# MoE weights fetched 1024 columns wide, its experts reordered into long stretches, the first expert's overflow slots packed

## The chip, the cores and the metric

The kernel runs on one core of a Trainium2 chip, in one launch. The metric is the device time in microseconds (us), here of that one core. Engines are named as the profile names them: PE is TensorE (PEld its weight loads), DVE VectorE, ACT ScalarE, POOL GpSimd, SP SyncE, which issues nearly all weight loads.

## What is computed

A block of two layers runs on 256 tokens of width 1024, all in float32; a second block of two layers follows. The first block has SwiGLU layers around a mixer of delta rule, convolution and attention. The second has a short convolution, a SwiGLU, a dilated attention and last a mixture of experts (MoE). Every normalisation of the second block is shifted and scaled by vectors that come from `silu(c) @ mod_w` ("modulation"). The change lies in the MoE, with one edit in the modulation:

```python
def swiglu_2(h, w_gate, w_up, w_down):
    return (jax.nn.silu(h @ w_gate) * (h @ w_up)) @ w_down

def moe_swiglu(h, w_router, w_gate, w_up, w_down):      # 8 experts, each 1024 -> 2816 -> 1024
    top_val, top_idx = lax.top_k(h @ w_router, 2)       # every token goes to two experts
    ...
    for e in range(N_EXPERTS):
        out = out + gates[..., e:e + 1] * swiglu_2(h, w_gate[e], w_up[e], w_down[e])
```

## The kernel before

**Weights and precision.** Outside the Half experts (below) a float32 product is made of fp32r matmuls: a weight piece of 128x1024 is split into `wh` (a copy, ACT, L197) and `wl` (the rest, DVE, L198) by `Core.parts`; the activations are split likewise. `mm3` then adds three matmuls: high by high, high by low, low by high. Activations are the stationary operand, weights the moving one. `Core.load` (L175) fetches up to 1 MB of weights per DMA (L187) on SP's queue into a ring of buffers, six of 1 MB in the MoE (`K.more(3)` adds three to three); `parts` writes into a ring of four pairs.

**The experts.** `Experts.route` ranks the eight experts by how many tokens chose them, on the chip; position 0 is the fullest, 7 the emptiest. `Experts.gather` (L1629) picks the tokens of up to three positions with one-hot matmuls. Three sorts of work follow.
- `Slots` (positions 0 to 3): up to 128 tokens, three fp32r matmuls of 512 columns per 128 rows of weight and 512 columns.
- `Half` (positions 4 to 7, and the tokens of position 0 beyond 128): up to 64 tokens. Its weights are not split; `halves` (L254) issues two plain fp32 matmuls with 64 stationary columns, which write rows 0 to 63 and rows 64 to 127 of one PSUM bank. The trace shows each as two records. The result lies as two halves of the columns, one under the other, and `feat` (L1454) copies and transposes gate and up, each on its own.
- An `If` at the end for counts beyond these.

`Experts.expert` (L1675) runs one position: for every 512 of the 2816 columns the gate products, then the up products (`proj_tok`, L259: loads of 4x128 rows by 512 columns, so rows of 2 KB), then `rows` (L303) for the down product (loads of 2x128 rows by 1024 columns, rows of 4 KB). It is a generator, which yields after each column chunk and after each down load. The PSUM banks are seven for products (`acc`) and one for transposes (`tr`).

**The order.** `moe` (L1691) writes the order of work with `beside`, which alternates two generators: position 0 (with its overflow) beside 7 and then 6; position 1 beside 5; position 2 beside 4; position 3 alone. So three of the four stages mix a Slots expert with a Half one, changing over after every chunk and, in the down products, after every load. Inside position 0 the Slots matmuls and the Half matmuls of the overflow alternate at every 128x1024 piece. The framework orders each engine's instructions by a simulated time line that starts from this order, so the trace shows the order it chose; each engine then runs its list in that order.

**The modulation.** `modulation` (L1128) is stepped once per weight load in three of the first block's SwiGLU stages. For each 512 of its columns it loads four pieces of `mod_w` on POOL's queue, adds them up on DVE (`macc`), and, right after the fourth (`k0 == 6`), splits the sum into `mh` and `ml` and sums it over the partitions with two matmuls into the bank `pm`; there are 24 such groups.

Of the kernel before, what the change touches and what calls it, by code (L numbers as in the profile page):

```python
# [18 lines left out]
P = 128  # L19
# [68 lines left out]
class Core:  # L88
# [170 lines left out]
    def proj_tok(self, xs, W, c0, n, kts, done, also=()):  # L259


# [4 lines left out]
        for k0 in range(0, kts, kc):  # L266
            m = min(kc, kts - k0)
            w = self.load([W[k0 * P:(k0 + m) * P, c].rearrange("(k p) n -> p k n", p=P) for c in cols], m, n)
            for j0 in range(0, m, kp):
                piece = w[:, j0:min(m, j0 + kp)]  # L270
                split = [] if self.raw(xs) else self.parts(piece)
                for t, x in enumerate(xs):
                    for j in range(piece.shape[1]):
                        k = k0 + j0 + j
                        ends = k == 0, k == kts - 1
                        if isinstance(x, Raw):
                            self.halves(ps[t], x(k), piece[:, j], n // 2, *ends)
                        else:
                            self.product(ps[t][:, :n], x, k, [v[:, j] for v in split], *ends)
        for t, x in enumerate(xs):  # L280
            done(t, ps[t][:, :n // 2 if isinstance(x, Raw) else n])
# [846 lines left out]
def modulation(K, part):  # L1128
# [19 lines left out]
    ahead = load(*pieces[0])  # L1148
    yield
    for n, (r, c0, k0) in enumerate(pieces):  # L1150
# [16 lines left out]
        if k0 == 6:  # L1167
            h, l = (pool.tile([P, 512], F32R, name=x, bufs=1) for x in ("mh", "ml"))
            K.split(acc, h, l)
            ps = K.bank("pm")  # L1170
            K.mm(ps, one, h, True, False)
            K.mm(ps, one, l, False, True)
            out = acc[0:1]
            nc.vector.tensor_tensor(out, ps[0:1], vec[:, 0], op=ALU.add)
            if j == 1:
                nc.vector.scalar_tensor_tensor(out, out, 1.0, vec[:, 1], op0=ALU.add, op1=ALU.mult)
            nc.gpsimd.dma_start(K.mods[r:r + 1, c0:c0 + 512], out)
        if n % 2:
            yield

# [200 lines left out]
class Slots:  # L1381
# [13 lines left out]
    def gate(self, ps, n):  # L1395
        self.g = self.E.tmp.tile([P, 512], F32, tag="sg", name="sg")
        self.nc.scalar.activation(self.g[:, :n], ps, AF.Silu)

    def up(self, ps, n, k0):
        K, m = self.K, n // P  # L1400
        self.nc.vector.tensor_tensor(self.g[:, :n], self.g[:, :n], ps, op=ALU.mult)
        tp = heads(K.tr(), 4)
        for j in range(m):
            K.transpose(tp[:, j], self.g[:, j * P:(j + 1) * P])
        K.split(tp[:, :m], self.h[:, k0:k0 + m], self.l[:, k0:k0 + m])

    def down(self, ps):
# [3 lines left out]
        for half in range(2):  # L1411
            c = slice(half * 512, half * 512 + 512)
            y = ps[half]
            if E.ending:
                y = E.tmp.tile([P, 512], F32, tag="sg", name="y")
                nc.vector.tensor_tensor(y, ps[half], E.scale[:, c], op=ALU.mult)
            K.split(y, yh[:, c], yl[:, c])
        pm, tp = E.tmp.tile([P, 2, P], F32, tag="pmd", name="pmd", bufs=1), heads(K.tr(), 4)
        for t in range(2):
            E.onehot(pm[:, t], self.slot, t, self.pos)  # L1420
            K.transpose(tp[:, t], pm[:, t])
        pt = E.tmp.tile([P, 2, P], F32R, tag="pt", name="pt")
# [8 lines left out]
        E.fresh = False  # L1431

# [10 lines left out]
class Half(Slots):  # L1443
# [20 lines left out]
    def gate(self, ps, n):  # L1464
        g = self.E.tmp.tile([P, 256], F32, tag="hg", name="hg")[:, :n // 2]
        self.g = g.rearrange("p (h j s) -> p h j s", h=2, s=64)
# [345 lines left out]
```

## Time and profile before

| | us |
|---|---|
| median of 3 runs (2684.63 to 2686.72) | 2685.23 |
| the profiled execution's own time | 2684.64 |
| its span, first to last instruction | 2682.8 |
| PE busy in the span | 2584.4 (96%) |
| DVE busy | 1738.8 (65%) |
| ACT busy | 1226.8 (46%) |

HBM read is 630.18 MB, 235 GB/s over the span. How to read a profile of this kind: busy time is the union of the records of an engine; matmuls are pipelined, so a record is longer than the step from one start to the next, and the step is what an engine's pace is read from. A wait line says which engine stood idle and what ended it. A window line has, for a stretch of time, the busy time of each engine with its number of records, the granted TensorE clock, the mean busy share of the 16 DMA engines and the GB/s moved. A few matmul records can be missing.

### The profile page before, as it was taken

The page shows a single profiled execution, that of the slowest core. Times are in us where ns is not written, and L with a number is a line of the kernel's source. Part 1 is how long each engine was busy: PE and PEld are TensorE (multiplying, and loading weights), DVE is VectorE, ACT ScalarE, POOL GpSimd, SP SyncE. Part 2 cuts the span into 40 slices and gives each one's busy share as a digit, 9 for nine tenths or more (in the row PEclk, how much of TensorE's full clock was granted, in tenths as well). Part 3 has the DMA queues.
Part 4 walks back from the last instruction along what each step waited for, and adds up shares of the span by engine and source line. Part 5 has one row for each costly group of instructions (what it writes and reads, how often), then busy time and mean ns, then how long its engine had stood idle before and what let it go on. Part 6 is the DMA issues. An engine that isn't in the chain of part 4 may idle for free. (4 is left out here: it accounts for less than half of the span.)

```text
span 2682.8 us, 37809 instructions
## 1 busy us (share of the span) xinstructions
PE 2584.4 (96%) x14817; PEld 2069.5 (77%) x14817; DVE 1738.8 (65%) x2490; ACT 1226.8 (46%) x1771; POOL 168.4 (6%) x259
## 2 busy tenths in 40 slices
PE   8999999999999999999999999997999999999997
PEld 6889999777778899988879788785556556666566
DVE  7868798887786688875556554765333355455487
ACT  5436545444444564454435443453322234434466
POOL 1210100122120010000000000001000000000000
PEclk9999999999999999999999999998999999999999
DMA  8865435787786552456555555424887989999995
GB/s 320 288 240 171 127 111 161 247 283 274 252 287 222 169 160 81 153 182 215 180 190 195 181 188 188 144 78 177 328 336 280 336 317 381 362 364 363 370 344 204
DMA packets 310678, 633.82 MB, mean 236 GB/s; under 512 B 16428, under 2 KB 107548, under 8 KB 310492
## 3 DMA queue, kind: packets, MB, share of 16 engines
q1 hardware_dynamic: 294876, 580.87, 61.6%
q0 software_dynamic: 15616, 50.46, 5.6%
q8 instruction: 118, 1.93, 0.3%
q14 instruction: 68, 0.56, 0.1%
HBM read 630.18 MB, written 1.10 MB: 235 GB/s over the span
## 5 line engine op out<-in xcount | busy, mean ns | idle before, releaser
L198 DVE TENSOR_TENSOR wl<-w,wh 128x1024 fp32r<-128x1024 f32 (+2 forms) x818 | 976.2, 1208 | 440.0 <-ACT wh L197 436.2
L197 ACT ACTIVATE wh<-w 128x1024 fp32r<-128x1024 f32 (+2 forms) x818 | 842.8, 1047 | 699.9 <-PE acc L202 539.2
L202 PE MATMUL acc<-wh,xh 128*128 128x512 f32 (+4 forms) x1584 | 605.6, 384 | 9.7 <-ACT xh L215 4.2
L202 PE MATMUL acc<-wl,xh 128*128 128x512 f32 (+4 forms) x1584 | 607.2, 383 | 7.3 <-DVE wl L198 7.2
L202 PE MATMUL acc<-wh,xl 128*128 128x512 f32 (+4 forms) x1584 | 600.0, 380 | 6.3 <-DVE xl L216 6.1
L202 PEld LDWEIGHTS acc<-wh,xh 128*128 128x128 f32 x1584 | 304.2, 192 | 79.6 <-issue 10.7
L202 PEld LDWEIGHTS acc<-wl,xh 128*128 128x128 f32 x1584 | 304.6, 192 | 73.8 <-DVE wl L198 13.7
L202 PEld LDWEIGHTS acc<-wh,xl 128*128 128x128 f32 x1584 | 304.8, 192 | 61.2 <-DVE xl L216 10.2
L202 PE MATMUL acc<-xh,wl 128*128 128x256 f32 x864 | 247.4, 286 | 0.0
L202 PE MATMUL acc<-xh,wh 128*128 128x256 f32 x864 | 247.1, 286 | 0.0
L202 PE MATMUL acc<-wl,ah 128*128 128x512 f32 x616 | 246.8, 401 | 0.3 <-DVE wl L198 0.3
L202 PE MATMUL acc<-xl,wh 128*128 128x256 f32 x864 | 245.4, 284 | 0.0
L202 PE MATMUL acc<-wh,al 128*128 128x512 f32 x616 | 241.9, 394 | 0.0
L202 PE MATMUL acc<-wh,ah 128*128 128x512 f32 x616 | 230.6, 398 | 0.0
L202 PE MATMUL acc<-w,xr 128*64 128x256 f32 (+1 forms) x1920 | 229.9, 367 | 0.0
L202 PEld LDWEIGHTS acc<-w,xr 128*64 128x64 f32 x1920 | 131.1, 136 | 78.0 <-issue 31.6
L202 PEld LDWEIGHTS acc<-xh,wh 128*128 128x128 f32 x864 | 165.4, 191 | 0.7 <-issue 0.5
L202 PEld LDWEIGHTS acc<-xl,wh 128*128 128x128 f32 x864 | 165.1, 191 | 0.6 <-issue 0.5
L202 PEld LDWEIGHTS acc<-xh,wl 128*128 128x128 f32 x864 | 165.1, 191 | 0.1
L1166 DVE SCALAR_TENSOR_TENSOR macc<-wm,vec,macc 128x512 f32<-128x512 f32 x168 | 125.1, 745 | 46.4 <-DMA wm<-in_mod_w_dram 45.0
L202 PEld LDWEIGHTS acc<-wl,ah 128*128 128x128 f32 x616 | 115.8, 188 | 50.3 <-issue 13.5
L202 PEld LDWEIGHTS acc<-wh,ah 128*128 128x128 f32 x616 | 114.4, 188 | 33.0 <-ACT wh L197 4.1
(414 smaller groups left out, 2749.5 us busy)
## 6 DMA issues: line engine op xcount, KB each, us to landing
w<-in_moe_w_gate_dram SPq DMA_DIRECT2D x88, 1024.0 KB
w<-in_moe_w_up_dram SPq DMA_DIRECT2D x88, 1024.0 KB
w<-in_moe_w_down_dram SPq DMA_DIRECT2D x88, 1024.0 KB
w<-in_ffn_w_gate_dram SPq DMA_DIRECT2D x55, 1024.0 KB
w<-in_ffn_w_up_dram SPq DMA_DIRECT2D x55, 1024.0 KB
w<-in_ffn_w_down_dram SPq DMA_DIRECT2D x55, 1024.0 KB
wm<-in_mod_w_dram POOLq DMA_DIRECT2D x96, 512.0 KB, 5.8
w<-in_w_in_dram SPq DMA_DIRECT2D x48, 1024.0 KB
```

What stands on the lines that cost most here:

```text
L197: self.nc.scalar.activation(like(h), v, AF.Copy)
L198: self.nc.vector.tensor_tensor(like(l), v, like(h).bitcast(F32), op=ALU.subtract)
L202: self.nc.tensor.matmul(out=out, lhsT=l, rhs=r, start=start, stop=stop)
L1166: nc.vector.scalar_tensor_tensor(acc, w[:, k], sc, acc, op0=ALU.mult, op1=ALU.add)
```

## The change

It has five parts.
1. `wide` takes the place of `proj_tok` in the experts: gate and up go in chunks of 1024, 1024 and 768 columns, loads of 2x128 rows by 1024 (or 768) columns, so rows of 4 KB (3 KB). A Slots job takes two PSUM banks for a chunk, a Half job one.
2. `Half` applies silu to the bank of the gate product as it lies, multiplies by the bank of the up product, and transposes the product once, up to four blocks in a bank, instead of gate and up apart, two blocks in a bank.
3. The overflow of position 0 is `Packed`: its 64 token columns of high part and 64 of low part stand side by side as one stationary operand of 128 columns, so that two fp32r matmuls (by `wh` and by `wl`) of 512 columns take the place of four fp32 records; `feat` then transposes and adds the two halves of the rows.
4. The order: position 0 with its overflow still alternates with 7 and 6, but by chunks of gate or of up (4 MB) and by four down loads; then 5, 1, 2, 3 and 4 run one behind the other. There are five gathers instead of four.
5. In `modulation` the two `pm` matmuls of a group and what follows them move to the next group's second piece (`k0 == 2`), and the small vectors are loaded at `k0 == 4`. Some scratch tiles share tags ("sg" with three buffers).

```diff
+    def wide(self, xs, W, c0, n, done):
+        pieces = [[slice(0, n // 2)] if isinstance(x, Raw) else [slice(c, min(n, c + 512)) for c in range(0, n, 512)]
+                  for x in xs]
+        ps = [[self.acc()[:, :c.stop - c.start] for c in cs] for cs in pieces]
+        for k0 in range(0, 8, 2):
+            w = self.load(W[k0 * P:(k0 + 2) * P, c0:c0 + n].rearrange("(k p) n -> p k n", p=P), 2, n)
+            split = [] if self.raw(xs) else [self.parts(w[:, j:j + 1]) for j in range(2)]
+            for x, cs, out in zip(xs, pieces, ps):
+                for j in range(2):
+                    k = k0 + j
+                    ends = k == 0, k == 7
+                    if isinstance(x, Raw):
+                        self.halves(out[0], x(k), w[:, j], n // 2, *ends)
+                    else:
+                        for c, o in zip(cs, out):
+                            self.product(o, x, k, [v[:, 0, c] for v in split[j]], *ends)
+        for t in range(len(xs)):
+            done(t, ps[t])
...
+    def rest(r, c0, vec, h, l, out):
+        ps = K.bank("pm")
+        K.mm(ps, one, h, True, False)
+        K.mm(ps, one, l, False, True)
+        nc.vector.tensor_tensor(out, ps[0:1], vec[:, 0], op=ALU.add)
+        if r % 3 == 1:
+            nc.vector.scalar_tensor_tensor(out, out, 1.0, vec[:, 1], op0=ALU.add, op1=ALU.mult)
+        nc.gpsimd.dma_start(K.mods[r:r + 1, c0:c0 + 512], out)
...
         if k0 == 0:
             acc = pool.tile([P, 512], F32, name="macc", bufs=2)
+        if k0 == 2 and left:
+            rest(*left)
+        if k0 == 4:
...
             K.split(acc, h, l)
-            ps = K.bank("pm")
-            K.mm(ps, one, h, True, False)
-            K.mm(ps, one, l, False, True)
...
+            left = r, c0, vec, h, l, acc[0:1]
         if n % 2:
             yield
+    rest(*left)
...
 class Slots:
...
+    def gate(self, banks):
+        self.g = []
+        for ps in banks:
+            g = self.E.tmp.tile([P, 512], F32, tag="sg", name="sg", bufs=3)[:, :ps.shape[-1]]
+            self.nc.scalar.activation(g, ps, AF.Silu)
+            self.g.append(g)
+
+    def up(self, banks, k0):
+        K = self.K
+        for g, ps in zip(self.g, banks):
+            m = ps.shape[-1] // P
+            self.nc.vector.tensor_tensor(g, g, ps, op=ALU.mult)
+            tp = heads(K.tr(), 4)
+            for j in range(m):
+                K.transpose(tp[:, j], g[:, j * P:(j + 1) * P])
+            K.split(tp[:, :m], self.h[:, k0:k0 + m], self.l[:, k0:k0 + m])
+            k0 += m
...
 class Half(Slots):
...
-    def feat(self, ps, n):
-
-        K, m = self.K, n // 2
-        r = self.E.tmp.tile([P, 256], F32, tag="hr", name="hr")
-        self.nc.scalar.activation(r[:, :m], ps, AF.Copy)
+    def gate(self, banks):
+        ps, = banks
+        self.g = self.E.tmp.tile([P, 512], F32, tag="sg", name="sg", bufs=3)[:, :ps.shape[-1]]
+        self.nc.scalar.activation(self.g, ps, AF.Silu)
+
+    def up(self, banks, k0):
+        K, (ps,) = self.K, banks
+        m = ps.shape[-1] // P
+        self.nc.vector.tensor_tensor(self.g, self.g, ps, op=ALU.mult)
         tp = heads(K.tr(), 4)
-        for j in range(m // P):
-            K.transpose(tp[:, j], r[:, j * P:(j + 1) * P])
-        return tp[:, :m // P].rearrange("p j (h s) -> p h j s", h=2)
-
-    def gate(self, ps, n):
-        g = self.E.tmp.tile([P, 256], F32, tag="hg", name="hg")[:, :n // 2]
-        self.g = g.rearrange("p (h j s) -> p h j s", h=2, s=64)
-        self.nc.scalar.activation(self.g, self.feat(ps, n), AF.Silu)
-
-    def up(self, ps, n, k0):
-        d = self.s[:, k0:k0 + n // P].rearrange("p (h j) s -> p h j s", h=2)
-        self.nc.vector.tensor_tensor(d, self.g, self.feat(ps, n), op=ALU.mult)
+        for j in range(m):
+            K.transpose(tp[:, j], self.g[:, j * P:(j + 1) * P])
+        d = self.s[:, k0:k0 + 2 * m].rearrange("p (h j) s -> p h j s", h=2)
+        self.nc.scalar.activation(d, tp[:, :m].rearrange("p j (h s) -> p h j s", h=2), AF.Copy)
...
+class Packed(Slots):
+
+
+    def __init__(self, E, x, slot, pos, tags):
+        self.tags = tags
+        super().__init__(E, x, slot, pos)
+
+    def room(self):
+        self.s = [self.E.t(n, DFF // P // 2, P, dt=F32R) for n in self.tags]
+        return (lambda k: self.at(k)[:, 0],)
+
+    def at(self, k, n=1):
+        half = DFF // P // 2
+        return self.s[k // half][:, k % half:k % half + n]
+
+    def feat(self, ps, tag, bufs):
+
+        K, nc, n = self.K, self.nc, ps.shape[-1]
+        m = n // P
+        r = self.E.tmp.tile([P, 512], F32, tag="sg", name="r", bufs=3)
+        nc.scalar.activation(r[:, :n], ps, AF.Copy)
+        tp = heads(K.tr(), 4)
+        for j in range(m):
+            K.transpose(tp[:, j], r[:, j * P:(j + 1) * P])
+        f = self.E.tmp.tile([P, 4, 64], F32, tag=tag, name=tag, bufs=bufs)[:, :m]
+        nc.scalar.activation(f, tp[:, :m, 64:], AF.Copy)
+        nc.vector.tensor_tensor(f, tp[:, :m, :64], f, op=ALU.add)
+        return f
+
+    def gate(self, banks):
+        self.g = [self.feat(ps, "pg", 2) for ps in banks]
+        for g in self.g:
+            self.nc.scalar.activation(g, g, AF.Silu)
+
+    def up(self, banks, k0):
+        for g, ps in zip(self.g, banks):
+            u = self.feat(ps, "pu", 1)
+            self.nc.vector.tensor_tensor(u, u, g, op=ALU.mult)
+            for j in range(ps.shape[-1] // P):
+                d = self.at(k0)
+                self.K.split(u[:, j:j + 1], d[:, :, :64], d[:, :, 64:])
+                k0 += 1
+
+    def onehot(self, pm, t):
+        for c in (0, 64):
+            self.E.onehot(pm[:, t, c:c + 64], self.slot, t, self.pos)
+
...
 class Experts:
...
-        for c0 in range(0, DFF, 512):
-            n = min(512, DFF - c0)
-            K.proj_tok(xs, wg, c0, n, 8, lambda t, ps: jobs[t].gate(ps, n))
-            K.proj_tok(xs, wu, c0, n, 8, lambda t, ps: jobs[t].up(ps, n, c0 // P))
-            yield n // 64
-        yield from K.rows([j.a for j in jobs], wd, DFF // P, lambda t, ps: jobs[t].down(ps))
+        for c0 in range(0, DFF, 1024):
+            n = min(1024, DFF - c0)
+            K.wide(xs, wg, c0, n, lambda t, banks: jobs[t].gate(banks))
+            yield n // P
+            K.wide(xs, wu, c0, n, lambda t, banks: jobs[t].up(banks, c0 // P))
+            yield n // P
+        n = 0
+        for m in K.rows([j.a for j in jobs], wd, DFF // P, lambda t, ps: jobs[t].down(ps)):
+            n += m
+            if n == 8:
+                yield n
+                n = 0
+        yield n
...
 def moe(K, x, y, scale, result):
...
-        main0, extra0, half7 = E.gather([(0, E.slot, E.room(0, x01)), (0, E.beyond, E.room(0)), (7, E.slot, E.room(1))])
-
-        def beside(heavy, light, share, late=lambda: None):
-
-            ahead, done = 0, 0
-            while heavy or light:
-                if heavy and (ahead <= 0 or not light):
-                    n = next(heavy, 0)
-                    heavy, ahead = heavy if n else None, ahead + share * n
-                else:
-                    n = next(light, 0)
-                    light, ahead, done = light if n else None, ahead - n, done + n
-                    if late and done > 11:
-                        late, _ = None, late()
-
-        later = {}
-
...
+        main, extra, half7 = E.gather([(0, E.slot, E.room(0, x01)), (0, E.beyond, x01[0][:, :, P:]),
+                                       (7, E.slot, E.room(0))])
+        jobs = {7: half7}
+
+        def gather(*what):
+            for pos, start in zip((pos for pos, _ in what), E.gather([(pos, E.slot, room) for pos, room in what])):
+                jobs[pos] = start
 
         def lights():
-            yield from E.expert(7, [half7])
-            second()
-            yield from E.expert(6, [later["x"][1]])
-
-        beside(E.expert(0, [main0, extra0]), lights(), 2, None)
+            yield from E.expert(7, [jobs[7]])
+            gather((6, E.room(1)), (5, E.room(2)))
+            yield from E.expert(6, [jobs[6]])
+
+
+        heavy, light, ahead = E.expert(0, [main, extra]), lights(), 0
+        while heavy or light:
+            if heavy and (ahead <= 0 or not light):
+                n = next(heavy, 0)
+                heavy, ahead = heavy if n else None, ahead + 2 * n
+            else:
+                n = next(light, 0)
+                light, ahead = light if n else None, ahead - n
         E.scale = scale(E.big)
-        beside(E.expert(1, [later["x"][0]]), E.expert(5, [later["x"][2]]), 1, third)
-        beside(E.expert(2, [later["y"][0]]), E.expert(4, [later["y"][1]]), 1, fourth)
-        E.end()
-        most = nc.values_load(E.most[0:1, 0:1], min_val=-P, max_val=SEQ + 64)
-        for _ in E.expert(3, later["z"]):
-            pass
+        for pos, later in ((5, ((1, E.room(0, x01)), (4, E.room(0)))), (1, ((2, E.room(1, x01)),)),
+                           (2, ((3, E.room(0, x01)),)), (3, ()), (4, ())):
+            if pos == 4:
+                E.end()
+                most = nc.values_load(E.most[0:1, 0:1], min_val=-P, max_val=SEQ + 64)
+            for _ in E.expert(pos, [jobs[pos]]):
+                if later:
+                    gather(*later)
+                    later = ()
```

## Rows read from the trace of the kernel before

**Rows 1.** The page's slices: busy tenths of PE and of the DMA engines, 40 slices.

```profile
PE   8999999999999999999999999997999999999997
...
DMA  8865435787786552456555555424887989999995
```

**Rows 2.** Windows, the MoE's four stages: engines' busy us, clock, DMA share, GB/s.

```profile
1846.00:2166.00 320.00, 316.73 (x1926) 180.56 (x1927) 104.21 (x140) 97.05 (x157) 1.25 (x3) 1.00 0.88 319
2166.00:2365.00 199.00, 193.44 (x1036) 124.02 (x1034) 101.42 (x114) 83.41 (x111) 0.42 (x1) 0.97 0.96 361
2365.00:2562.00 197.00, 187.32 (x1009) 122.93 (x1007) 99.26 (x104) 85.25 (x111) 0.00 (x0) 0.97 0.98 364
2562.00:2666.00 104.00, 99.86 (x461) 80.30 (x460) 94.92 (x98) 73.79 (x79) 0.00 (x0) 1.00 0.80 291
```

**Rows 3.** Waits of SP's queue, 1860 to 2150, then 2560 to 2660: total, times, longest.

```profile
SPq L187 <- PE acc L202: 221.7, 80, 12.4
...
SPq L187 <- DVE wl L198: 69.6, 27, 8.7
```

**Rows 4.** Timeline of PE, 1872 to 1900 us: start, duration, what, count.

```profile
1872.40 0.66 PE L223 MATMUL tr<-const,sg 128*128 128x128 f32 x4
1872.99 4.54 PE L202 MATMUL acc<-w,xr 128*64 128x256 f32 x40
1877.45 0.44 PE L223 MATMUL tr<-const,hr 128*128 128x128 f32 x2
1877.82 3.67 PE L202 MATMUL acc<-w,xr 128*64 128x256 f32 x32
...
1894.62 0.40 PE L202 MATMUL acc<-wl,xh 128*128 128x512 f32 x1
1894.86 0.39 PE L202 MATMUL acc<-wh,xl 128*128 128x512 f32 x1
1895.17 1.08 PE L202 MATMUL acc<-w,xr 128*64 128x256 f32 x8
1896.19 0.50 PE L202 MATMUL acc<-wh,xh 128*128 128x512 f32 x1
1896.53 0.40 PE L202 MATMUL acc<-wl,xh 128*128 128x512 f32 x1
```

**Rows 5.** Groups of instructions by line and shape, 1840 to 2683 us.

```profile
L202 PE MATMUL acc<-w,xr 128*64 128x256 f32 x1600 | 208.0, 385 | 0.0
...
L202 PE MATMUL acc<-w,s 128*64 128x512 f32 x440 | 112.7, 603 | 0.0
...
L1458 ACT ACTIVATE hr<-acc 128x256 f32<-128x256 f32 x50 | 19.1, 381 | 156.3 <-PE acc L202 152.4 <-PE tr L223 3.9
...
L1471 DVE TENSOR_TENSOR s<-hg,tr 128x256 f32<-128x256 f32 x25 | 10.5, 419 | 69.5 <-PE tr L223 65.4 <-ACT wh L197 4.2
```

**Rows 6.** Groups by line and shape, 2562 to 2666 us (position 3 alone).

```profile
L198 DVE TENSOR_TENSOR wl<-w,wh 128x1024 fp32r<-128x1024 f32 x65 | 77.2, 1220 | 6.1 <-ACT wh L197 5.5
```

**Rows 7.** Page, DMA issues: what, count, KB each.

```profile
w<-in_moe_w_gate_dram SPq DMA_DIRECT2D x88, 1024.0 KB
```

**Rows 8.** Windows (columns as in rows 2): gate and up loads, down loads, a clock drop.

```profile
2220.00:2250.00 30.00, 30.00 (x196) 21.28 (x195) 14.77 (x23) 12.32 (x22) 0.00 (x0) 1.00 1.01 375
2340.00:2370.00 30.00, 29.19 (x120) 15.60 (x119) 12.80 (x12) 11.31 (x13) 0.00 (x0) 1.00 1.03 411
2272.00:2280.00 8.00, 6.25 (x28) 4.01 (x29) 4.77 (x5) 5.13 (x7) 0.00 (x0) 0.80 1.05 396
```

**Rows 9.** Waits of PE and of PEld, 0 to 1845 us: the modulation's bank.

```profile
PE pm L202 <- DVE ml L216: 4.9, 3, 2.4
...
PE pm L202 <- ACT mh L215: 1.6, 2, 0.8
...
PEld pm L202 <- DVE ml L216: 7.2, 5, 2.7
...
PEld pm L202 <- ACT mh L215: 3.5, 5, 1.2
```

More of the change, by code (lines that the diff above doesn't have):

```diff
@@ L269, in proj_tok @@
             for j0 in range(0, m, kp):
-                piece = w[:, j0:min(m, j0 + kp)]
-                split = [] if self.raw(xs) else self.parts(piece)
+                wh, wl = self.parts(w[:, j0:min(m, j0 + kp)])
                 for t, x in enumerate(xs):
-                    for j in range(piece.shape[1]):
+                    for j in range(wh.shape[1]):
                         k = k0 + j0 + j
-                        ends = k == 0, k == kts - 1
-                        if isinstance(x, Raw):
-                            self.halves(ps[t], x(k), piece[:, j], n // 2, *ends)
-                        else:
-                            self.product(ps[t][:, :n], x, k, [v[:, j] for v in split], *ends)
-        for t, x in enumerate(xs):
-            done(t, ps[t][:, :n // 2 if isinstance(x, Raw) else n])
+                        self.product(ps[t][:, :n], x, k, (wh[:, j], wl[:, j]), k == 0, k == kts - 1)
+        for t in range(len(xs)):
+            done(t, ps[t][:, :n])
+    def wide(self, xs, W, c0, n, done):
[14 more added lines that the diff above has]
+                            self.product(o, x, k, [v[:, 0, c] for v in split[j]], *ends)
+        for t in range(len(xs)):
+            done(t, ps[t])
     @staticmethod
@@ L1147, in modulation @@
             yield
-    ahead = load(*pieces[0])
+    ahead, left = load(*pieces[0]), None
     yield
+    def rest(r, c0, vec, h, l, out):
[6 more added lines that the diff above has]
+        nc.gpsimd.dma_start(K.mods[r:r + 1, c0:c0 + 512], out)
     for n, (r, c0, k0) in enumerate(pieces):
@@ L1510, in __init__ @@
         self.K, self.nc, self.x, self.y, self.fresh, self.ending = K, K.nc, x, y, True, False
-        self.half = 0
         self.big = es.enter_context(K.tc.tile_pool(name="moe", bufs=1, reuse_waits="tile"))
@@ L1649, in gather @@
                     ks, p = slice(k0, k0 + 2), ps[:, :, c]
-                    if isinstance(x, tuple):
-                        d = x[part][:, ks]
+                    if isinstance(x, tuple) or x.dtype == F32R:
+                        d = x[part][:, ks] if isinstance(x, tuple) else x[:, ks, part * 64:part * 64 + 64]
                         if part:
@@ L1664, in start @@
             return lambda: Slots(self, tuple((lambda k, a=a: a[:, k]) for a in x), slot, pos)
-        self.half += 1
-        tag = f"s{self.half % 3}"
-        return lambda: Half(self, Raw(lambda k: x[:, k]), slot, pos, tag)
+        if x.dtype == F32R:
+            return lambda: Packed(self, (lambda k: x[:, k],), slot, pos, ("p0", "p1"))
+        return lambda: Half(self, Raw(lambda k: x[:, k]), slot, pos, f"s{pos % 2}")
     def room(self, i, xT=None):
@@ L1719, in moe @@
-        later = {}
-        def second():
-            later["x"] = E.gather([(1, E.slot, E.room(1, x01)), (6, E.slot, E.room(2)), (5, E.slot, E.room(3))])
-        def third():
-            later["y"] = E.gather([(2, E.slot, E.room(0, x01)), (4, E.slot, E.room(0))])
-        def fourth():
-            later["z"] = E.gather([(3, E.slot, E.room(1, x01))])
-        def lights():
-            yield from E.expert(7, [half7])
-            second()
-            yield from E.expert(6, [later["x"][1]])
@@ L1753, in moe @@
                         pass
-        K.spare = E.big, "s1", DFF // 2
+        K.spare = E.big, "s0", DFF // 2
         for t in range(2):
```

38 lines of the change are left out of this document (12 added, 26 removed).

## The prediction

> **What bounds the kernel now.** I read the page first: PE is busy in nearly every slice, and in the last third, the MoE, the DMA engines are nearly full as well [rows 1]. An average over both can't say which one sets the pace, so I cut the MoE into its four stages by the groups of matmuls that run in them [rows 2]: position 0 with 7 and 6 (1846 to 2166, 320 us), 1 with 5 (199 us), 2 with 4 (197 us), 3 alone with the end (104 us), 820 us together. In the first, PE is busy 316.7 of 320 us and DMA has 12% to spare. In the second and third the DMA share is 0.96 and 0.98. In the last DVE is busy 94.9 of 104 us and PE 99.9, with DMA at 0.80. So the stages have different bounds: PE, DMA, DMA, then PE and DVE. SP's waits agree: in the first stage the weight buffers come free when matmuls end (221.7 us of waiting), in the last when DVE's splits end (69.6 us) [rows 3].
>
> A busy PE is not PE at its peak, so I read steps from the timeline [rows 4]. An fp32r matmul of 512 columns starts 0.24 us after the one before it. Forty Half records of 256 columns take 1872.99 to 1877.45, 0.112 us each: the two half arrays run side by side. Where the two kinds alternate there is loss: from the start at 1894.86 to the one at 1896.53 are 1.67 us, and one matmul (0.24), eight Half records (0.89) and one matmul (0.24) would take 1.37. **A change there and back costs 0.30 us.** Two transposes among Half records take 0.37 us of the stream (1877.45 to 1877.82), four 0.59 us (1872.40 to 1872.99). And DMA: with loads of 2 KB rows it moves 375 GB/s at share 1.01, with 4 KB rows 411 at 1.03 [rows 8].
>
> **The change part by part.** The sum stands against the profiled execution's own 2684.6 us (its span of 2682.8 and 1.8 around it), 0.6 under the median of the three runs.
>
> *Modulation.* The two `pm` matmuls now come a weight load after the split they read. PE stood idle for `ml` and `mh` 4.9 + 1.6 us, its weight loads 7.2 + 3.5 [rows 9]; the former is in the latter to an unknown part. I take 6.5 us off, with 0 and 12 as ends: the nearest row is PE's own. The moved step's DMA (`mods`) and its vector loads go on POOL's queue a load later; who waits for them is a stage later by hundreds of us, so they cost nothing. The piece loads behind them have the next piece already fetched as cover; without it DVE would wait for `wm`, which lies inside the 12.
>
> *First stage (position 0 with 7 and 6).* Removed: position 0 has 44 gate and up pieces and 22 down pieces, and before each gave a change to the overflow's Half matmuls and back, 66 x 0.30 = 19.8 us. Packed stays among full-width matmuls. Its matmuls cost the same: two of 512 columns (0.48) for four Half records (0.45). Transposes: the three Half jobs had 12 blocks of mostly two, 36 x 0.37 = 13.3 us; now two jobs have 3 blocks of mostly four, 6 x 0.59 = 3.5, and Packed 12 blocks of about 0.45 (between the two rows), 5.4: 4.4 us less. Changes between position 0 and 7 or 6 fall from some 17 to some 9, 2 us. Together 26 us; of this I take **20**, since part of any gap is filled by a wait that follows. Packed's copies, adds and splits are not in this trace. By the nearest groups, 0.38 us (L1458) and 0.42 (L1471) per operation [rows 5], some 50 of them on ACT and 40 on DVE make less than 20 us each, on engines busy 97 and 104 of 320 us [rows 2]: hidden, and if that cover failed they would give the whole 20 back. With one transpose bank, its chain of copy, transpose, copy, add is what would be late next. After it this stage needs 300 us, and its 3 x 34.6 MB at 411 GB/s 253: still PE's.
>
> *The rest (500 us now).* Each expert is 33 MB-loads [rows 7], 34.6 MB, so 84 us at 411 GB/s. A Half expert alone needs of PE 320 records x 0.112 (1600 over five jobs), 64 narrow ones at half of that, and 88 (440 over five) at twice: 59 us [rows 5], with transposes and scatter about 64. It is thus DMA's. But the Slots expert before it is slower than DMA, so the ring of six buffers stands full when it starts; (34.6 - 6.3) MB at 411 is 69 us, taken as 70. There are two such, 5 and 4: 140 us. A Slots expert alone needs 396 matmuls of 512 columns at 0.235, 93 us, on PE, and 66 splits at 1.22 us (80.5) [rows 6] and some 14 us more on DVE. The last stage shows it measured: 104 us with about 5 us of its neighbours' scatter and its own tail [rows 2], so 99. Three are 297 us. Gathers between them (three, one more than now) 2.5 us each on PE, 7.5; last scatter 4. Sum 448.5: **51 us less**. The wider rows earn their part here: with the ring and 375 GB/s the two Half experts would take 75 each. The two or three extra loads per expert (35 for 33) go unnoticed on SP, which mostly waits. The last expert is now a Half one, and ends soon after its last load.
>
> In this sum DMA beats 400 GB/s for 70 us at a stretch. The longest stretch near that in the rows is 30 us [rows 8]; the two DMA-bound stages averaged 361 and 364 [rows 2]. At 364 sustained the two Half experts would take 78 us each, 16 us more in all, and that lies in the range.
>
> The Trainium skill, "DMA: Bandwidth & Descriptors", section Specifications, speaks against it: it gives a core about 358 GB/s of HBM. By that the five experts' 173 MB need 483 us and the rest of the MoE gains 17, an estimate from the page's figure. The trace does not agree: it shows 411 GB/s over 30 us [rows 8].
>
> Sum: 6.5 + 20 + 51 = 77.5; 2684.6 - 77.5 = **2607 us**.
>
> **The rivals.**
> 1. *A sustained DMA ceiling.* The 361 and 364 GB/s of the mixed stages are what the memory gives over long times, wider rows only lift short bursts, and a ring that is never refilled gives no head start. Then the rest runs at that rate from end to end: 5 x 34.6 = 173 MB at 364 are 475 us for 500, 25 gained in place of 51, and 2684.6 - 6.5 - 20 - 25 = 2633 us. For it: share 0.98 at 364. Against: in those stages two thirds of the bytes came in 2 KB rows, and 411 was reached in the others. Chance 0.15. By the Trainium skill's figure above it would be 2641, an estimate.
> 2. *The stretches cancel.* Mixing let the Slots expert's DVE and PE work lie beside the Half expert's DMA; alone, each shows its own bound. If the ring's head start is lost at each boundary (Half 85 to 88 each) and Slots alone takes the whole 104, the rest is 2 x 87 + 312 + 11 = 497, no gain; first stage and modulation remain: 2658 us. For it: 3 alone ran DMA at only 0.80. Chance 0.12.
> 3. *Slower: the clock falls in the Half experts alone.* PE there has 64 us of work in 70, and gaps after each load. In 2272 to 2280 PE was busy 6.25 of 8 us and the granted clock averaged 0.80, between its levels of 2.4 and 1.2 GHz [rows 8]. If the clock sat low for all of positions 5 and 4, PE would need 128 us for each, 116 more in all than the 2607: 2723 us. It decides the sign when about two thirds of the two are at the low level. Against: at 1.2 GHz PE is full again, and in the rows the low level is short. Chance 0.06.
> 4. *The order does not come out.* The simulated time line may still mix the jobs on PE, and save only what it removes elsewhere: about 2682. Against: the trace before follows the written order at the scale of chunks. Chance 0.05.
>
> **How the numbers follow.** My forecast has 0.62, with a range of its own of 2590 to 2625. The time is its own, 2607. Low end: 12 for the modulation, 30 for the first stage, 62 for the rest, if Slots experts take 96: 2580. High end takes in rivals 1 and 2: 2660. Within 0.2% (5 us, about what a measurement tells from no change) lies rival 4, 0.05; slower, rival 3, 0.06; faster the rest, 0.89.
>
> **What would show it.** First stage near 300 us, with Half records in blocks of dozens and no change at every piece. Positions 5 and 4 alone, with DMA share above 1.0, over 400 GB/s, and PE idle for loads; about 70 us each. Positions 1, 2, 3 at 96 to 100 us each, DVE over 90% busy. PE no longer waiting for `ml`. Wrong would be: GB/s under 370 in the Half experts (rival 1), Slots experts over 104 us or Half over 85 (rival 2), a clock well under 1.0 there (rival 3).

## The result and the profile after

The changed kernel takes 2649.55 us (median of 4 runs, 2647.32 to 2650.85), the kernel before 2685.97 beside it: ratio 0.9861, 95% interval 0.9844 to 0.9878. The gain is 36 us where 77.5 were forecast; the time lies inside the range. The profiled execution took 2649.65 us (span 2647.8).

The page's slices of the changed kernel, to be held against [rows 1]:

```profile
PE   8999999999999999999999999997999998999995
PEclk9999999999999999999999999997999999999998
DMA  8875335687887453456557455531987889999997
```

A slice is 66.2 us. PE has a slice of 8 at 2184 to 2250 us, which is position 5, and ends with one of 5, position 4 and the close; the DMA engines stand at 9 from 2184 to 2581. For a closer look the MoE needs cuts at its own borders. I take the router's first `acc<-sel,const` matmul as its start and the last scatter matmul (`acc<-s,pt`, `acc<-ah,pt`) of a job as a stage's end; a stretch below is the stage of one position alone. The timeline of PE before shows that the first stage did not end at 2166, where [rows 2] cut it, but when position 1's first product starts:

```profile
2178.47 1.03 PE L202 MATMUL acc<-w,s 128*64 128x512 f32 x4
...
2185.52 2.05 PE L202 MATMUL acc<-s,ptz 128*128 128x512 f32 x6 [0.30 <-DVE z L1440]
2187.50 0.50 PE L202 MATMUL acc<-wh,xh 128*128 128x512 f32 x1
```

By these borders, windows of the kernel before (first stage; 1 with 5; 2 with 4; 3; columns as in [rows 2]):

```profile
1833.20:2187.20 354.00, 345.33 (x2044) 197.71 (x2044) 123.24 (x207) 106.40 (x171) 1.25 (x3) 0.99 0.86 315
...
2187.00:2376.60 189.60, 183.20 (x992) 120.67 (x992) 98.12 (x110) 82.09 (x109) 0.42 (x1) 0.96 0.97 366
2376.60:2567.00 190.40, 181.36 (x992) 119.83 (x990) 96.66 (x102) 81.78 (x105) 0.00 (x0) 0.97 0.98 363
2567.00:2668.00 101.00, 98.14 (x454) 78.90 (x452) 91.42 (x94) 72.22 (x77) 0.00 (x0) 1.00 0.78 280
```

and of the changed kernel (first stage; then 5, 1, 2, 3, 4):

```profile
1836.30:2170.20 333.90, 315.14 (x1465) 193.52 (x1466) 126.32 (x233) 106.51 (x178) 0.84 (x2) 0.97 0.86 331
...
2170.00:2251.00 81.00, 70.39 (x338) 24.77 (x337) 8.72 (x21) 8.57 (x18) 0.00 (x0) 1.00 0.97 381
2251.00:2356.00 105.00, 103.63 (x498) 85.25 (x497) 94.97 (x102) 79.54 (x93) 0.00 (x0) 1.00 0.99 381
2356.00:2457.00 101.00, 100.55 (x488) 83.36 (x487) 90.62 (x95) 78.17 (x91) 0.00 (x0) 1.00 0.93 344
2457.00:2555.60 98.60, 97.26 (x455) 77.41 (x454) 82.26 (x85) 70.63 (x80) 0.42 (x1) 1.00 0.93 343
2555.60:2632.50 76.90, 62.98 (x288) 19.85 (x287) 11.77 (x19) 4.60 (x8) 0.00 (x0) 1.00 0.91 366
```

First stage: 354.0 to 333.9 us. All that lies behind it: 480.7 to 462.3. The start of the MoE: 1833.2 to 1836.3, later. Together -20.1, -18.4 and +3.1, which is the 35 us between the two profiles. The mean granted clock of 0.96 and 0.97 in the mixed stages before has become 1.00; in the first stage it went from 0.99 to 0.97, and PE stands idle there for 18.8 us where it did for 8.7.

The same cuts in every profile (us):

| kernel | first stage | behind it | of which |
|---|---|---|---|
| before | 354.0 | 480.7 | 1 with 5: 189.4, 2 with 4: 190.4, 3: 100.9 |
| after | 333.9 | 462.3 | 5: 80.8, 1: 105.4, 2: 100.5, 3: 98.8, 4: 76.9 |
| e1_mod_only | 353.9 | 477.5 | 187.9, 188.7, 100.9 |
| e2_mod_back | 335.5 | 461.0 | 79.5, 105.4, 100.5, 98.8, 76.8 |
| e3_no_packed | 349.9 | 461.2 | 80.1, 105.4, 100.5, 98.8, 76.4 |
| e4_mixed | 337.0 | 466.1 | 1 with 5: 185.4, 2 with 4: 181.6, 3: 99.1 |
| e5_rows2k | 336.1 | 464.5 | 81.9, 105.3, 100.5, 98.8, 78.0 |
| e6_late_gathers | 335.9 | 461.7 | 5: 78.6, 1: 104.3, 2: 98.8, 4: 76.5, 3: 103.5 |
| e7_busy_half | 333.9 | 464.1 | 81.3, 105.4, 100.5, 98.8, 78.1 |
| e8_ring5 | 345.2 | 466.7 | 82.8, 105.3, 100.5, 98.8, 79.3 |
| e9_ring7 | 328.6 | 457.0 | 78.3, 105.3, 100.5, 98.8, 74.1 |
| e10_ring7_late | 327.9 | 455.7 | 77.0, 104.3, 100.5, 98.8, 75.1 |
| e11_order_only | 352.7 | 465.7 | 83.6, 103.8, 100.4, 97.5, 80.3 |

Where the code of a stage is the same, it repeats within 0.1 us for a Slots stretch, 1.3 for a Half stretch, 1.7 for a mixed stage (before and e1) and 3 for the first stage. The total repeats less well, since the MoE's start alone lies between 1829.7 and 1842.2 us.

### The profile page after: what moved, and what is told of

Its sections match the earlier page's. It is cut to its first block, busy times and chain, and to the rows that moved or that the text cites. A ratio compares the mean times of both kernels' runs of the same rounds, so it can differ in the third digit from the quotient of the medians.

```text
span 2647.8 us, 36053 instructions
## 1 busy us (share of the span) xinstructions
PE 2528.1 (95%) x13865; PEld 2039.8 (77%) x13865; DVE 1744.0 (66%) x2531; ACT 1232.5 (47%) x1774; POOL 168.0 (6%) x258
## 5 line engine op out<-in xcount | busy, mean ns | idle before, releaser
L198 DVE TENSOR_TENSOR wl<-w,wh 128x1024 fp32r<-128x1024 f32 (+3 forms) x834 | 975.0, 1188 | 369.8 <-ACT wh L197 364.7
L197 ACT ACTIVATE wh<-w 128x1024 fp32r<-128x1024 f32 (+3 forms) x834 | 848.2, 1033 | 677.1 <-PE acc L202 551.1
L202 PE MATMUL acc<-wl,xh 128*128 128x512 f32 (+3 forms) x1680 | 630.1, 378 | 1.2 <-DVE wl L198 1.2
L202 PE MATMUL acc<-wh,xh 128*128 128x512 f32 (+3 forms) x1680 | 598.6, 379 | 9.4 <-ACT xh L215 4.9
L202 PEld LDWEIGHTS acc<-wh,xh 128*128 128x128 f32 x1680 | 316.1, 191 | 69.5 <-ACT xh L215 8.6
L202 PEld LDWEIGHTS acc<-wl,xh 128*128 128x128 f32 x1680 | 319.6, 190 | 60.3 <-DVE wl L198 3.0
L202 PE MATMUL acc<-w,xr 128*64 128x512 f32 (+1 forms) x768 | 165.4, 563 | 8.9 <-DMA w<-in_moe_w_up_dram 7.5
L202 PEld LDWEIGHTS acc<-wh,al 128*128 128x128 f32 x616 | 115.7, 188 | 26.8
```

Of the source, the lines that this page charges most:

```text
L197: self.nc.scalar.activation(like(h), v, AF.Copy)
L198: self.nc.vector.tensor_tensor(like(l), v, like(h).bitcast(F32), op=ALU.subtract)
L202: self.nc.tensor.matmul(out=out, lhsT=l, rhs=r, start=start, stop=stop)
```

## The experiments

**e1, e2: the modulation alone, and all but the modulation.** e1 is the kernel before with

```diff
+        if k0 == 2 and left:
+            rest(*left)
...
-            ps = K.bank("pm")
...
+            left = r, c0, vec, h, l, acc[0:1]
```

and e2 the changed kernel without it.

> The kernel before with the modulation edit alone. Theory (the two parameter loads and the store of a finished row now stand on POOL's queue ahead of the next weight load, which then comes late; VectorE and TensorE stall once and the clock dips): 2 to 4 us slower than before, about 2689, and the first routing matmuls of the experts start 2 to 3 us later than at 1826.3. Rival (the term of the prediction: TensorE's waits for ml, mh and macc at the two pm lines go): 6.5 us faster, about 2679.5, start at about 1820.

> The changed kernel with the modulation of before. Theory (the edit costs time): about 2647, 2 to 4 us faster than the changed kernel's 2649.6. Rival (the edit gives the 6.5 us of the prediction and some other part takes more than the trace shows): about 2656.

e1: 2684.64 us, ratio 0.9995 (0.9986 to 1.0004), so between 3.8 us faster and 1.1 slower. e2: 2651.53, ratio 0.9878 (0.9859 to 0.9896), beside the changed kernel's 0.9861. Neither is the 6.5 us of the prediction, nor 3 us of loss: both theories fall. The start of the MoE was at 1833.2, 1838.5 and 1840.1 us with the old modulation and at 1829.7 to 1842.2 in ten profiles with the new one. Why nothing came is in the waits of PE and of PEld in the changed kernel, beside [rows 9]:

```profile
PE pm L202 <- DVE ml L216: 4.9, 3, 2.4
...
PE pm L202 <- ACT mh L215: 1.4, 2, 1.2
```

```profile
PEld pm L202 <- DVE ml L216: 6.5, 4, 2.7
```

The waits are still there: 4.9 us for `ml`, the same as before. The timeline of the changed kernel shows one of these places:

```profile
603.40 0.75 DVE L1195 SCALAR_TENSOR_TENSOR macc<-wm,vec,macc 128x512 f32<-128x512 f32 x1 [2.09 <-DMA wm<-in_mod_w_dram]
...
606.72 0.50 PE L202 MATMUL pm<-mh,one 128*128 128x512 f32 x1 [1.24 <-ACT mh L215]
```

The adding up of the group waits 2.09 us for its own load (`wm`), so the split follows late, and PE still comes to the matmul before the split is done.

**e3: Packed taken out.** Position 0's overflow is a Half job again (with one more work buffer, and its own tile `s2`):

```diff
-(0, E.beyond, x01[0][:, :, P:])
+(0, E.beyond, E.room(3))
```

> The changed kernel with position 0's overflow as a Half tile again beside its Slots tile, in place of Packed; 1024-column loads, order and transposes stay. Theory (each change between full-width and half-width matmuls costs some 0.15 us one way, and Packed took away about 60 of each direction): the first stage grows by 14 to 20 us, total 2664 to 2670, and the changes between the two kinds in it go from about 10 to about 60 or more. Rival (the first stage's gain came from the 1024-column pieces and fewer transposes, Packed only moved work): total within 6 us of 2649.6.

2661.88 us (2654.28 to 2669.8), ratio 0.9904 (0.9884 to 0.9924): 12.3 us above the changed kernel, where 14 to 20 were expected. In the profile the first stage takes 349.9 us, 16.0 more, or 13 by the longest first stage of the runs that share the changed kernel's code there (337.0); nothing behind it changes. In PE's timeline the changes from full to half width and back are 63 and 61, in the changed kernel 11 and 9. The time between starts there beyond a regular step of 0.23 us adds up to 24 us against 7.5. The rival falls and the theory holds in the main: Packed is most of the first stage's gain.

**e4: the pairs alternated again**, in wide pieces: 1 with 5 and 2 with 4 in steps of 4 MB, 3 alone at the end.

```diff
+        beside(E.expert(1, [jobs[1]]), five, 1, ((2, E.room(1, x01)),), -n)
+        beside(E.expert(2, [jobs[2]]), E.expert(4, [jobs[4]]), 1, ((3, E.room(0, x01)),))
```

> The changed kernel with positions 1 and 5, then 2 and 4, alternated in steps of 4 MB, then 3 alone; 1024-column loads and Packed stay. Theory (a Half expert alone is bound by its 35 loads at 2.45 us and leaves TensorE idle a fifth of the time, a Slots expert alone is bound by TensorE and leaves the queue idle, so the order one behind the other gives away what mixing would overlap): 12 to 30 us faster than the changed kernel, 2620 to 2638. Rival 1 (mixing has a price of its own, the changes between kinds and waits for the slower partner, as large as the overlap): within 6 us of 2649.6. Rival 2 (the order is what brought the gain behind the first stage): the pairs go back to 199 and 197 us as in before, about 2680.

2655.14 us, ratio 0.9888 (0.987 to 0.9906). My theory falls, and rival 2 with it; rival 1 stands: the pairs take 185.4 and 181.6 us where one behind the other takes 186.2 and 177.4. Windows of the two mixed stages:

```profile
2171.80:2357.20 185.40, 179.47 (x835) 112.06 (x834) 105.59 (x121) 86.83 (x110) 0.42 (x1) 0.98 0.96 373
...
2357.20:2538.80 181.60, 172.80 (x789) 103.47 (x788) 94.16 (x104) 80.29 (x98) 0.42 (x1) 0.99 1.00 386
```

What mixing costs is seen best in the timeline of PE in the kernel before, where it goes from position 5's matmuls to position 1's:

```profile
2272.26 1.95 PE L202 MATMUL acc<-w,xr 128*64 128x256 f32 x16
2274.69 0.44 PE L223 MATMUL tr<-const,hr 128*128 128x128 f32 x2 [0.48 <-ACT hr L1458]
2275.63 0.50 PE L202 MATMUL acc<-wh,xh 128*128 128x512 f32 x1 [0.51 <-ACT wh L197]
2276.89 0.79 PE L202 MATMUL acc<-wl,xh 128*128 128x512 f32 x1 [0.76 <-DVE wl L198]
2277.48 0.63 PE L202 MATMUL acc<-wh,xl 128*128 128x512 f32 x1
2277.91 0.63 PE L202 MATMUL acc<-wh,xh 128*128 128x512 f32 x1
...
2280.38 0.39 PE L202 MATMUL acc<-wh,xh 128*128 128x512 f32 x1
2280.61 0.39 PE L202 MATMUL acc<-wl,xh 128*128 128x512 f32 x1
```

Three short waits, 1.75 us together: for a transpose's input, then for the first split of the other job. Then matmuls start 0.43 us apart in place of 0.23, for some 3 us: TensorE runs at its lower level, 1.2 of 2.4 GHz (granted clock 0.80 in 2272 to 2280, [rows 8]). Half jobs need no splits, so it seems that none lie ready when a Slots job takes over. By the mean clocks, the two mixed stages before lost at most 0.04 x 189.6 + 0.03 x 190.4 = 13.3 us to this, e4 0.02 x 185.4 + 0.01 x 181.6 = 5.5, the changed kernel about nothing. "At most", because e1 runs the same MoE code as the kernel before and met fewer such drops:

```profile
2190.30:2378.20 187.90, 180.50 (x992) 118.11 (x990) 98.38 (x110) 82.74 (x109) 0.42 (x1) 0.98 0.98 371
2378.20:2566.90 188.70, 179.65 (x991) 118.55 (x990) 96.38 (x102) 81.80 (x105) 0.00 (x0) 0.98 0.98 366
```

By the same reckoning it lost 0.02 x 187.9 + 0.02 x 188.7 = 7.5 us, 5.8 less, but its mixed stages are only 3.2 us shorter.

**e11: the order alone**, in the kernel before with its pieces of 512 columns.

```diff
-        beside(E.expert(1, [later["x"][0]]), E.expert(5, [later["x"][2]]), 1, third)
-        beside(E.expert(2, [later["y"][0]]), E.expert(4, [later["y"][1]]), 1, fourth)
...
+            for _ in E.expert(pos, [job()]):
+                if late:
+                    late, _ = None, late()
```

> The kernel before with the order of the change alone: first stage as before, then 5, 1, 2, 3, 4 one behind the other, in its pieces of 512 columns. Behind the first stage before took 481 us, the changed kernel 462, and the changed kernel with the pairs alternated 466. Theory 1 (pieces and order are two cures for the same loss, TensorE's stops at each change of kind and the clock's dips, so either alone gives most of it): 465 to 470 us behind the first stage, total 2670 to 2675. Theory 2 (they add up: the order is worth the 4 us between 466 and 462, the pieces the 15 between 481 and 466): 476 to 478, total about 2681. The first stage as before, 354 us, in both.

2674.7 us, ratio 0.9952 (0.9936 to 0.9968). Behind the first stage 465.7 us: theory 1. Windows of 5 and 1, then of 2, 3 and 4, the last few us by themselves:

```profile
2192.80:2380.20 187.40, 173.83 (x1004) 120.42 (x1003) 103.17 (x115) 90.16 (x115) 0.42 (x1) 1.00 1.01 378
2380.20:2655.00 274.80, 261.79 (x1423) 193.25 (x1421) 183.94 (x190) 153.43 (x181) 0.00 (x0) 1.00 0.96 352
2655.00:2658.50 3.50, 3.00 (x7) 2.33 (x8) 1.30 (x2) 0.45 (x1) 0.00 (x0) 0.60 0.04 9
```

The clock is back at 1.00 up to the last few us. So the order alone gives 15 us, wide pieces in the old alternation 14.6, and both together 18.4: the two gains overlap and do not add up. The clock's part is common to both. The changes between full and half width are not: counted as in e3 they take 12 us in the mixed stages before, 1 in e11, but 17 in e4. What else is in the 14.6 us was not taken apart.

**e5: 2 KB rows.** Each gate and up load is issued in two column halves.

```diff
-            w = self.load(W[k0 * P:(k0 + 2) * P, c0:c0 + n].rearrange("(k p) n -> p k n", p=P), 2, n)
+            w = self.load([W[k0 * P:(k0 + 2) * P, c:min(c + 512, c0 + n)].rearrange("(k p) n -> p k n", p=P)
+                           for c in range(c0, c0 + n, 512)], 2, n)
```

> The changed kernel with each gate and up load of 1 MB issued as two transfers of 512 columns (rows of 2 KB in memory in place of 4 KB); nothing else moves. Theory (the row's length sets what the queue moves: 2 KB rows 365 GB/s in the pairs of before, 4 KB rows 375 to 380 in the alternated pairs and 416 in a Half stretch): each Half stretch grows by 4 to 8 us from 80.8 and 76.9, the Slots stretches, which TensorE bounds, by at most 2 each, the total by 10 to 18. Rival (bytes alone count, the 4 KB rows gave nothing): every stretch within 1 us of the changed kernel's, total within 3.

2655.3 us, ratio 0.9902 (0.9877 to 0.9927). The total is 5.8 us above the changed kernel's, between the theory's 10 to 18 and the rival's 3. The Half stretches grow by 1.1 us each, the Slots stretches not at all; the 2.2 us more in the first stage lie within its spread, and 1.1 us is no more than a Half stretch varies by. That is well under the theory's 4 to 8 and near the rival. Windows of e5 in 5's gate and up loads, then in its down loads, which kept their 4 KB rows:

```profile
2195.00:2222.00 27.00, 26.07 (x114) 9.00 (x110) 0.69 (x1) 2.28 (x4) 0.00 (x0) 1.00 1.06 397
2222.00:2250.00 28.00, 22.05 (x95) 6.33 (x95) 1.04 (x3) 1.09 (x2) 0.00 (x0) 1.00 1.03 415
```

Wide rows move 415 GB/s where narrow ones move 397; the changed kernel's own windows of 10 us in 5's gate and up loads from 2190 on move 408 and 412. So narrow rows are slower while they are read, but little of it reaches the stretch.

**e7: VectorE and ScalarE kept busy in the Half stretches**, by splits of half the rows that nobody reads.

```diff
+            if len(xs) == 1 and self.raw(xs) and self.idle:
+                self.parts(w[:, 0:1])
...
+                    if not j and len(xs) == 1 and self.raw(xs) and self.idle:
+                        self.parts(w[:, 0:1])
```

> The changed kernel with splits that nobody reads added in the two Half stretches: of each load of 1 MB one of the two row blocks is split by ScalarE and VectorE (about 1.06 and 1.22 us per 2.45). Theory (VectorE and ScalarE at work slow the queue's packets, which is why 4 KB rows moved 416 GB/s in a Half stretch, 375 to 380 in the alternated pairs and 347 to 372 in a Slots stretch): the rate in the middle of 5's and 4's stretch falls to 380 to 390 and the DMA share stays at 1.0, each stretch grows by 4 to 6 us. Rival (the lower rates came from the loads waiting for free buffers, not from the engines): the rate stays at 412 to 418, the stretches within 1 us of 80.8 and 76.9.

One profile, 2649.97 us. The middle of 5's stretch in e7, then in the changed kernel:

```profile
2200.00:2245.00 45.00, 36.44 (x171) 10.94 (x171) 23.47 (x25) 21.15 (x24) 0.00 (x0) 1.00 1.03 416
```

```profile
2200.00:2245.00 45.00, 36.69 (x174) 10.79 (x169) 1.73 (x4) 2.18 (x4) 0.00 (x0) 1.00 1.03 416
```

VectorE goes from 1.7 to 23.5 busy us of 45 and the rate stays at 416 GB/s: the rival holds. The 363 to 386 GB/s of the mixed stages, at a share of 0.96 to 1.00, were thus not a price of a busy VectorE and ScalarE. Nor was it one of TensorE: inside stage 1 with 5 of the kernel before, two windows of 8 us, PE full in both, stand far apart:

```profile
2307.00:2315.00 8.00, 8.00 (x92) 7.27 (x91) 3.12 (x4) 3.33 (x7) 0.00 (x0) 0.96 0.57 207
...
2339.00:2347.00 8.00, 8.00 (x34) 4.82 (x35) 3.99 (x4) 4.02 (x4) 0.00 (x0) 1.00 1.02 415
```

The mean of a stage hides such pauses of the queue.

**e8, e9: a ring of five and of seven loads.** `K.more(3)` becomes `K.more(2)` and `K.more(4)`. In e9 the space comes from one product tile for all Half jobs and from reusing Packed's tiles.

> The changed kernel with a ring of five loads in place of six. Theory (a Half stretch is 35 loads less those that stood ready in the ring, at 2.45 us each, as in the prediction): 5's and 4's stretch grow by about 2.5 us each, the Slots stretches by less than 1, the first stage by 0 to 3, total plus 4 to 8. Rival (the depth of the ring does not matter, the head start is lost while TensorE gathers and scatters): every stretch within 0.7 us.

> The changed kernel with a ring of seven loads in place of six; the space comes from one tile for all Half experts' products and from Packed's two tiles, used again after the first stage. Theory (a ring of five cost 2.0 and 2.4 us in the Half stretches and 11.3 us in the first stage, where TensorE runs into loads of the Half experts' down step, so a seventh load gives part of that back): 5's and 4's stretch 2 to 2.5 us shorter than 80.8 and 76.9, the first stage 3 to 8 us shorter than 333.9, the Slots stretches unchanged within 0.5, total 8 to 12 us less, 2638 to 2642. Rival (six was deep enough for the first stage): the first stage within 1.5 us, total 4 to 5 us less.

e8: 2659.2 us in one profile. The Half stretches grow by 2.0 and 2.4 us, as the theory has it, but the first stage by 11.3 (8 to 11 by its spread), which it had not. Its waits of PE there (the changed kernel has 4.0 us for `wh` and 3.0 for down loads):

```profile
PE acc L202 <- ACT wh L197: 8.3, 6, 2.1
PE acc L202 <- DMA w<-in_moe_w_down_dram: 6.3, 10, 1.5
```

e9: 2640.16 us, ratio 0.9837 (0.9817 to 0.9858), an interval that overlaps the changed kernel's. By stages its theory holds: the Half stretches shrink by 2.5 and 2.8 us, the first stage by 5.3 (6.0 in e10, which has the same ring), the Slots stretches by nothing. The first stage is PE's on average, yet its Half jobs are quicker than the queue. In 5's stretch of the changed kernel, the eight matmuls of a down load take 1.94 us and the next load lets PE start 2.47 us after the last:

```profile
2244.09 1.94 PE L202 MATMUL acc<-w,s 128*64 128x512 f32 x8 [0.50 <-DMA w<-in_moe_w_down_dram]
2246.56 1.94 PE L202 MATMUL acc<-w,s 128*64 128x512 f32 x8 [0.53 <-DMA w<-in_moe_w_down_dram]
```

So each step of 4 MB of a Half job draws the ring down, and where it runs dry PE stands still. That this is what the first stage's Half jobs meet as well is read from e8's waits for down loads.

**e6, e10: the gathers moved to where PE waits for loads.** e6 also puts position 3 last and has the gathers behind the fifth and seventh step; e10 is e9 with the order 5, 1, 2, 3, 4 kept. The lines are e10's.

```diff
+        one, two = ((1, E.room(0, x01)), (4, E.room(0))), ((2, E.room(1, x01)),)
+        for pos, later in ((5, {4: one, 7: two}), (1, {}), (2, {1: ((3, E.room(0, x01)),)}), (3, {}), (4, {})):
```

> The changed kernel with the order 5, 1, 2, 4, 3 and the gathers moved into the Half stretches, behind their fifth and seventh step, where TensorE waits for loads: those of 1, 2 and 4 into 5's, that of 3 into 4's. Theory (a gather at the head of a Half stretch holds TensorE while the ring is full, so the queue stops: 214 GB/s in 2170:2180; behind the fifth step it lies in a wait for a load, and a gather in a Slots stretch is plain TensorE time): 5's stretch 76 to 78 us against 80.8, 1's about 100 against 105.3, 2's about 98.5 against 100.5, 4's and 3's as before within 1.5; total 8 to 12 us faster, 2638 to 2642. Rival (the Half stretch has no slack that a gather can use, whatever its place: it adds its 4 us wherever it stands): 5's stretch 84 or more, total within 3 us of 2649.6.

> As e9_ring7, and the gathers for 1 and 4, then the one for 2, stand behind the fourth and the seventh step of 5's stretch; the order stays 5, 1, 2, 3, 4 and the gather for 3 stays in 2's stretch. Theory (three gathers in 5's stretch ended it 2.2 us earlier than two at its head, and 1's stretch was 1.1 us shorter without the gather for 2): 5's stretch 76 to 77.5, 1's 104 to 105, the rest as in e9_ring7, total 3 us less than e9_ring7. Rival (with a seventh load the head of 5's stretch no longer empties the queue, so the place of the gathers does not matter): 5's stretch within 1 us of e9_ring7's or longer.

e6: 2652.16 us, ratio 0.9873 (0.9854 to 0.9891), no gain. 5's stretch fell to 78.6 with one gather more in it, against the rival. But 1's gave only 1.1 us where 5 were expected: PE waits 3.1 us for `wl` there, in the changed kernel 0.8, so the gather had filled waits for the first splits. And 3 behind a Half job took 103.5 us where it had 98.8 behind a Slots job; here too PE waits 3.1 us for `wl`. So a Slots job that follows a Half one costs some 5 us more, and e6 has two such places.

e10: 2634.78 us, ratio 0.9822 (0.98 to 0.9844), the fastest of all; its interval meets the changed kernel's only at the end. 5's stretch is 77.0 us with three gathers, and 1's 104.3. Beside e9 this is little: 5's stretch is 1.3 us shorter, as much as such a stretch varies by, 1's 1.0 shorter, 4's 1.0 longer, and the 5.4 us between the two medians lie within the runs' range (2630.03 to 2646.21). Windows around the start of 5's stretch, in the changed kernel (from 2170.2) and in e10 (from 2157.6):

```profile
2170.00:2180.00 10.00, 10.00 (x57) 4.83 (x56) 3.47 (x8) 1.70 (x5) 0.00 (x0) 1.00 0.62 214
2180.00:2190.00 10.00, 10.00 (x55) 4.19 (x55) 2.56 (x9) 1.10 (x4) 0.00 (x0) 1.00 0.96 343
...
2230.00:2240.00 10.00, 7.62 (x34) 1.91 (x32) 0.00 (x0) 0.00 (x0) 0.00 (x0) 1.00 1.03 418
```

```profile
2157.00:2167.00 10.00, 10.00 (x47) 3.57 (x47) 2.63 (x4) 0.60 (x1) 0.00 (x0) 1.00 0.89 321
2167.00:2177.00 10.00, 9.14 (x46) 3.20 (x44) 0.69 (x1) 0.60 (x1) 0.00 (x0) 1.00 1.02 406
```

In the changed kernel PE scatters 0's rows and then gathers for 1 and 4 while the ring is full, and the queue stands still for want of a buffer: SP issues no load between 2162.9 and 2172.5.

## Why the prediction was right and wrong

**First stage, -20: right.** 354.0 to 333.9; over the profiles that share the code, 352.7 to 354.0 and 333.9 to 337.0, so 16 to 20. The changes were the right mechanism: e3 gives 13 to 16 of it back. Their price of 0.30 us was read at one place; counted as in e3 over the whole first stage before, 71 and 68 changes take 15.8 us, 0.23 there and back, and the trim from 26 to 20 made up for that. Packed's copies and adds hide only in part: PE waits 4.2 us for `pu`. And the stage is PE's only on average, since a seventh load shortens it (e9).

**The rest, -51: the step that failed, in two terms.** Measured -18.4.

*The 500 us from which it was counted.* The prediction cut at 2166 and gave the last 21 us of the first stage (downs, scatters) to the rest. From 2187.2 the rest before is 480.7 us. This took 19 us off the gain; the first stage's own term was a difference and did not suffer.

*The two Half experts at 70 us.* Measured 80.8 and 76.9. The rate was right: 416 GB/s at share 1.03 over 45 us, beside the 411 used. The ring's head start was there too: a load more or less moved a Half stretch by 2.0 to 2.8 us, about the 2.45 us of one load. But "(34.6 - 6.3) MB" over the rate leaves out two things. A full ring is of use only while buffers come free, and at 5's start PE did a scatter and a gather first: at the 417 GB/s of later windows the queue missed 2.0 + 0.7 MB in 2170 to 2190, 6.6 us. And the end, where the last down product, split and scatter follow the last load: from PE's start on that load (2246.56 and 2626.40) to the stage's end are 4.4 us in 5 and 6.1 in 4. With these, 70 becomes 81 for 5. The standstill is read from windows; moving the gathers (e6, e10) gave back 1.3 to 2.2 us of it. Slots were near: 304.7 us with their gathers, for 297 and 5. In sum 462.3 for 448.5, 14 us.

*The reading behind it.* "PE, DMA, DMA, then PE and DVE" was wrong for the two mixed stages. Their share of 0.96 to 0.98 looked like a full queue, but PE was busy 183.2 of 189.6 us, slowed by changes, short stops and the clock, and the queue had pauses. What the order's 15 us are made of stays open: the clock is at most 13.3 of them, and less by e1; the changes between widths are about 11; both together are more than the gain, and PE idles 9 us more in e11 than before. Neither was tried by itself. Nor did wide rows "earn their part" in the Half experts as priced: e5 puts that at about 1 us each, not 5.

**Modulation, -6.5: wrong.** Waits that the trace names for `ml` were taken as gone because the reading matmuls moved in the code. They stayed (behind `wm` in the place shown), and e1 bounds the whole edit at 3.8 us. POOL's queue in the moved step "cost nothing" within the same bound.

The four differences, 19 + 14 + 6.5 and 3 for the later start, are the 42 between 77.5 and 35.

**The rivals.** Rival 1, a ceiling of 364 GB/s, is refuted by 407 GB/s over 63 us (2187 to 2250 in the changed kernel). The Trainium skill's figure of about 358 GB/s ("DMA: Bandwidth & Descriptors", Specifications), which its row works out as half of a stack's 716 GB/s for each of two cores, does not bound these loads of a single core either. That the 2641 worked out from it came close is an accident of the two errors above. Rival 2 named the right weak spot, the boundary where a Half stretch begins, but priced Half at 85 to 88 and Slots at 104. It lay nearer to the truth than the forecast: 2658 against 2649.6. Rival 3 had the clock the wrong way round: it was low in the mixed stages and 1.00 in the Half ones. Rival 4 fell: the stretches stand apart in the profile.

## What to carry to other kernels

Cut stages where the trace shows the last instruction of one and the first of the next, before subtracting: 19 of the 42 us were lost there and not on the chip. When a stretch is priced as its loads less a ring's head start, add the time at its start in which nothing empties the buffers (a scatter, a gather) and the work behind the last load: here 11 of 81 us. And two edits to the same stretch need not add up, here 15 and 14.6 us alone and 18.4 together: try each alone before pricing the pair.

## What was not expected of the hardware

- A DMA share of 0.96 to 1.00 over a stage did not mean a full queue: loads in wide rows moved 373 to 386 GB/s at that share in e4 and 416 at 1.03 in a Half stretch, and a stage of share 0.97 before held windows of 207 and of 415.
- VectorE and ScalarE busy for half the time (23.5 and 21.2 of 45 us) took nothing from that 416.
- One load more or less in a ring of six moved a stage in which PE is busy over 90% of the time by 5 to 11 us, where that stage varies by 3 (one profile with five loads, two with seven).
